# Eight pairs of buffers for split weight parts instead of seven, in a two-layer fp32 block on one core

## The chip, the core and the metric

The kernel runs on one core of a Trainium2 chip. The metric is device time in microseconds (us), from one launch on the inputs of the reference. Times of several runs are given as a median with the lowest and the highest.

## What is computed

The reference is two layers of a hybrid block on an activation `x` of 256 rows by 1024 columns in float32. Cut to what matters:

```
def hybrid_layer(x, ...):
    proj = rms_norm(x, g_mix_norm) @ w_in
    m_qk, m_v, m_o, m_i, m_f, moba_qkv, cq, ckv, kpe = split(proj)
    hm = mlstm_chunkwise(...)            # 4 heads, chunks of 64
    ha = moba_attention(...)             # 4 heads of 64, one block of 256
    hl = causal_block_attention(...)     # 4 heads, latent q and k, v
    x = x + concat([hm, ha, hl]) @ w_out
    h2 = rms_norm(x, g_mlp_norm)
    return x + square(relu(h2 @ w_up)) @ w_down     # 1024 -> 4096 -> 1024
```

All weights are float32 and come from memory once; together with the small inputs the run reads 113 MB.

## The kernel before

Every large product is made from split operands. A float32 number is written as a high part in TensorE's reduced float32 format plus a low part, and `mm3` (L249 to L252) issues three matmuls for each product: high by high, low by high, high by low. In the profile they are lines 250, 251 and 252 (405, 407 and 410 where a first block is put in another order). So each weight has to be split on its way:

- `load` (L192 to L201) fetches a job of up to 2048 columns x 128 partitions (1 MB) into one of three `raw` buffers, on SyncE's queue.
- `stream` (L203 to L227) cuts the job into pieces of up to 1024 columns. ScalarE writes the high part `wh` (L217), VectorE the low part `wl` by a subtraction (L225). For every fourth `up` piece of the MLP, VectorE is spared: ScalarE writes the negated high part into `wl` (L220), and GpSimd issues a transfer that adds the weights from memory to it (L222).
- `dn_part` (L229) gives the pieces of the down projection. For the first 14 of its 16 blocks four matrices are used, a (512 columns), b, d and c (1024 each), where d and c are sums that VectorE makes (`tsum`, L238 to L240); seven products of them, in the order a, b, d, c, d, c, b, stand for eight. The last two blocks take two pieces, e and b.
- `weights` (L244) is called where a piece is used. It splits ahead of that use:

```
    def stream(i):
        while state["split"] < min(i + SPLIT_AHEAD + 1, len(pieces)):
...
                h = hlp.tile([128, PW], F32R, name="wh", tag="wh")
                lo = hlp.tile([128, PW], F32R, name="wl", tag="wl")
```

The pool `hlp` has `SPLIT_AHEAD + 1` buffers of each of `wh` and `wl` (4096 bytes a partition each), the pool `rawp` has `DMA_AHEAD + 1`. A piece can be split once the piece that had its buffers has been used for the last time.

A layer runs through stages (projections, three kinds of attention, the output projection) in an order written out in `ORDERS` (L30). The program gives the order in which stages are recorded; a scheduler then sets the order of the instructions on each engine, from its own model of their durations. Where one stage ends and the next begins, `last_rows` updates the halves of `xs` one by one (L940 after the output projection, L988 after the MLP), and `transposer` (L388) with `transposed` transposes them on TensorE into `xtp` (L384), which ScalarE and VectorE split into `xh` (L376) and `xl` (L378); `first_blocks` (L398) holds the first matmuls on them.

The MLP loop (L992 to L1039) runs over 16 blocks of 256 hidden columns. In each round two `up` pieces are used for one bank `up`, ScalarE takes relu (`rr`, L1009) and square (`us`, L1010), VectorE makes three sums (L1012 to L1014), ScalarE and VectorE split the result into `hrh` (L1019) and `hrl` (L1020), and TensorE makes the products of the block two rounds back (`LAG`), P1 to P7.

In the middle of a layer, `lkl` (L710) is the normalised latent key on VectorE, `ltp` (L721) its transposes on TensorE, `scr` (L748) a square on ScalarE that reads the bank of the projection `pp`, and `qkp` and `vp` are further projections.

Of the kernel before, what the change touches and what calls it, by code (L numbers as in the profile page):

```python
# [23 lines left out]
RW = 2048  # L24
PW = 1024
DMA_AHEAD = 2
SPLIT_AHEAD = 6
LAG = 2

ORDERS = [o.split() for o in ("""  # L30
# [108 lines left out]
def hybrid_kernel(ctx: ExitStack, tc: tile.TileContext, x: bass.AP, xt: bass.AP, pos: bass.AP,  # L139
# [5 lines left out]
    rawp = ctx.enter_context(tc.tile_pool(name="raw", bufs=DMA_AHEAD + 1))  # L145
    hlp = ctx.enter_context(tc.tile_pool(name="hl", bufs=SPLIT_AHEAD + 1))
    tb = ctx.enter_context(tc.tile_pool(name="tb", bufs=1))
# [55 lines left out]
    def stream(i):  # L203
        while state["split"] < min(i + SPLIT_AHEAD + 1, len(pieces)):
            _, pc, j, c, n = pieces[state["split"]]
            while state["dma"] < min(j + DMA_AHEAD + 1, len(jobs)):
                next(load(state["dma"]))
                state["dma"] += 1
            r = raw[j][:, c:c + n]
            if pc[0] == "dn":  # L210
                r = dn_part(j, pc[2])
            if j == 0:
                hl[state["split"]] = (r,)
            else:
                h = hlp.tile([128, PW], F32R, name="wh", tag="wh")
                lo = hlp.tile([128, PW], F32R, name="wl", tag="wl")
                A.activation(h[:, :n], r, AF.Copy)  # L217
                if pc[0] == "up" and pc[1] % 4 == 3:

                    A.activation(lo, h.bitcast(F32), AF.Copy, scale=-1.0)  # L220
                    m, o = jobs[j]
                    G.dma_start(lo, bass.AP(tensor=wts.tensor, offset=wts.offset + o + c, ap=[[m, 128], [1, n]]),  # L222
                                accum_op=OP.add)
                else:
                    V.tensor_sub(lo[:, :n], r, h[:, :n].bitcast(F32))  # L225
                hl[state["split"]] = (h, lo)
            state["split"] += 1  # L227
# [895 lines left out]
```

## Time and profile before

| what | value |
|---|---|
| median of 3 runs | 600.15 us (599.92 to 601.45) |
| the profiled execution's own time | 601.67 us |
| its span, first to last instruction | 599.9 us |
| granted TensorE clock | 1.00 in every stretch (2.4 GHz) |
| busy: TensorE, its weight loads, VectorE, ScalarE, GpSimd | 98%, 87%, 86%, 70%, 9% |
| chain that ended last: TensorE, DMA, VectorE, ScalarE | 81%, 7%, 6%, 4% |
| software-made transfers (GpSimd's queue) | 2304 packets, 8.39 MB |

The span is 1.8 us shorter than the execution's own time. Busy shares are means over stages: the MLP loop, which runs from about 140 to 300 us and from about 430 to 590 us, is denser on VectorE than the attention stages. Matmuls overlap their neighbours, so their printed durations are longer than their pace; the pace is read from the starts of neighbours. A wait in the lists is idle time of the engine that ended when the named work was done.

### The profile page before, as it was taken

What the parts mean: (1) busy time and instruction counts of PE and PEld (TensorE: products, weight loads), DVE (VectorE), ACT (ScalarE), POOL (GpSimd) and SP (SyncE); (2) the same over time, 40 slices, a digit from 0 to 9 for tenths busy, and PEclk for the clock granted to TensorE, in tenths of its full rate; (3) what the DMA queues carried; (4) which work ended last, traced back from release to release, by engine and by line L of the source; (5) the groups of instructions that cost most, each with busy time, mean ns of one, the idle gap of its engine ahead of it and who ended that gap; (6) DMA issues with size and microseconds to landing.
All of it is one profiled execution on the core that took longest, in us unless ns stands there. A gap on an engine that the chain in (4) does not pass through costs nothing.

```text
span 599.9 us, 10005 instructions
## 1 busy us (share of the span) xinstructions
PE 585.6 (98%) x3766; PEld 523.8 (87%) x3766; DVE 516.2 (86%) x951; ACT 418.7 (70%) x671; POOL 54.6 (9%) x107
## 2 busy tenths in 40 slices
PE   6998999999999999999999999999999999999997
PEld 5987878889998898989889897888899899998985
DVE  4789895767999999999788997785789999999975
ACT  4785785557877778768657787563687787778670
POOL 7972000000000000000000000000000000000000
PEclk9999999999999999999999999999999999999999
DMA  8786321464676777678537623326656786778631
GB/s 292 280 290 235 101 109 43 175 207 141 186 243 210 243 243 232 223 230 257 191 110 253 235 82 133 107 71 205 180 159 227 204 267 214 215 227 243 219 101 70
DMA packets 19632, 114.78 MB, mean 191 GB/s; under 512 B 2560, under 2 KB 3072, under 8 KB 7808
## 3 DMA queue, kind: packets, MB, share of 16 engines
q1 hardware_dynamic: 16992, 105.75, 50.5%
q0 software_dynamic: 2304, 8.39, 7.7%
q8 instruction: 29, 0.48, 0.3%
q14 instruction: 19, 0.16, 0.1%
q10 hardware_dynamic: 288, 0.02, 0.0%
HBM read 113.09 MB, written 1.05 MB: 190 GB/s over the span
## 4 chain that ended last, share of the span: by engine, by line
PE 81%; DMA 7%; DVE 6%; ACT 4%; issue 1%; SPq 0%; DVEq 0%
PE up L251 8%; PE up L250 8%; PE up L252 8%; PE P L252 7%; PE P L251 7%; PE P L250 7%; DMA wl<-in_wts_dram 5%; DVE wl L225 3%; PE acc L250 2%; PE acc L252 2%; PE acc L251 2%; ACT wh L217 2%; PE latp L562 2%; DMA raw<-in_wts_dram 1%; PE vp L251 1%
## 5 line engine op out<-in xcount | busy, mean ns | idle before, releaser
L217 ACT ACTIVATE wh<-raw 128x1024 fp32r<-128x1024 f32 (+2 forms) x196 | 190.1, 981 | 72.6 <-PE acc L251 18.8
L225 DVE TENSOR_TENSOR wl<-raw,wh 128x1024 fp32r<-128x1024 f32 (+4 forms) x180 | 200.5, 1120 | 35.3 <-ACT wh L217 31.0
L251 PE MATMUL up<-xh,wl 128*128 128x256 f32 x480 | 133.8, 279 | 1.0 <-DMA wl<-in_wts_dram 1.0
L250 PE MATMUL up<-xh,wh 128*128 128x256 f32 x480 | 133.4, 278 | 0.9 <-DVE xl L378 0.9
L252 PE MATMUL up<-xl,wh 128*128 128x256 f32 x480 | 132.9, 277 | 0.0
L251 PEld LDWEIGHTS up<-xh,wl 128*128 128x128 f32 x480 | 90.3, 188 | 3.2 <-DMA wl<-in_wts_dram 1.8
L250 PEld LDWEIGHTS up<-xh,wh 128*128 128x128 f32 x480 | 90.1, 188 | 2.5 <-issue 1.4
L252 PEld LDWEIGHTS up<-xl,wh 128*128 128x128 f32 x480 | 90.2, 188 | 0.0
L252 PE MATMUL P<-wl,hrh 128*128 128x512 f32 x228 | 89.9, 394 | 0.0
L251 PE MATMUL P<-wh,hrl 128*128 128x512 f32 x228 | 89.5, 393 | 0.0
L250 PE MATMUL P<-wh,hrh 128*128 128x512 f32 x228 | 88.7, 389 | 0.0
L225 DVE TENSOR_TENSOR wl<-tsum,wh 128x1024 fp32r<-128x1024 f32 x56 | 66.2, 1218 | 0.4 <-ACT wh L217 0.4
L217 ACT ACTIVATE wh<-tsum 128x1024 fp32r<-128x1024 f32 x56 | 56.3, 1046 | 2.8 <-PE P L252 1.5
L222 POOL DMA_DIRECT2D wl<-in_wts_dram x16 | 14.0, 874 | 482.1 <-ACT wl L220 400.8
L251 PEld LDWEIGHTS P<-wh,hrl 128*128 128x128 f32 x228 | 42.8, 188 | 8.8
L252 PEld LDWEIGHTS P<-wl,hrh 128*128 128x128 f32 x228 | 42.9, 188 | 8.6
L250 PEld LDWEIGHTS P<-wh,hrh 128*128 128x128 f32 x228 | 42.8, 188 | 8.4
L1009 ACT ACTIVATE rr<-up 128x512 f32<-128x512 f32 x32 | 19.1, 597 | 34.8 <-PE up L252 34.8
L1019 ACT ACTIVATE hrh<-us 128x896 fp32r<-128x896 f32 (+1 forms) x32 | 29.1, 910 | 16.4 <-DVE us L1014 16.4
L238 DVE SCALAR_TENSOR_TENSOR tsum<-raw 128x1024 f32<-128x1024 f32 x28 | 34.1, 1219 | 6.2 <-DMA raw<-in_wts_dram 6.2
L1020 DVE TENSOR_TENSOR hrl<-us,hrh 128x896 fp32r<-128x896 f32 (+1 forms) x32 | 33.3, 1040 | 2.0 <-ACT hrh L1019 2.0
L250 PE MATMUL acc<-wh,mh 128*128 128x512 f32 x64 | 25.6, 400 | 0.0
(368 smaller groups left out, 1141.6 us busy)
## 6 DMA issues: line engine op xcount, KB each, us to landing
raw<-in_wts_dram SPq DMA_DIRECT2D x91, 1024.0 KB, 4.9
wl<-in_wts_dram POOLq DMA_DIRECT2D x16, 512.0 KB, 7.5
raw<-in_wts_dram SPq DMA_DIRECT2D x2, 740.0 KB, 5.0
raw<-in_wts_dram SPq DMA_DIRECT2D x2, 576.0 KB, 5.4
xts<-in_xt_dram SPq DMA_DIRECT2D x4, 256.0 KB, 4.6
raw<-in_wts_dram SPq DMA_DIRECT2D x4, 256.0 KB, 4.9
xs<-in_x_dram SPq DMA_DIRECT2D x1, 1024.0 KB, 10.0
raw<-in_wts_dram SPq DMA_DIRECT2D x2, 512.0 KB, 3.5
```

Source lines behind the costliest of these rows:

```text
L217: A.activation(h[:, :n], r, AF.Copy)
L222: G.dma_start(lo, bass.AP(tensor=wts.tensor, offset=wts.offset + o + c, ap=[[m, 128], [1, n]]), accum_op=OP.add)
L225: V.tensor_sub(lo[:, :n], r, h[:, :n].bitcast(F32))
L238: V.scalar_tensor_tensor(t[:, :1024], r[:, :1024], -1.0, r[:, 512:1536], op0=OP.mult, op1=OP.subtract)
L250: T.matmul(o, lh, rh, start=start, stop=False, **kw)
L251: T.matmul(o, ll, rh, start=False, stop=False, **kw)
L252: T.matmul(o, lh, rl, start=False, stop=stop, **kw)
L562: T.matmul(first[b], part(b, k)[0], xts[:, k], start=k == 0, stop=k == KT - 1))
L1009: A.activation(r, up, AF.Relu)
L1019: A.activation(hh, src, AF.Copy)
L1020: V.tensor_sub(hlo, src, hh.bitcast(F32))
```

## The change

```
-SPLIT_AHEAD = 6
+SPLIT_AHEAD = 7
...
-    nc = _bacc.Bacc("TRN2", target_bir_lowering=False, num_devices=1)
+    nc = _bacc.Bacc("TRN2", target_bir_lowering=False, num_devices=1, dynamic_dma_scratch_size=8192)
```

The pool of split parts gets an eighth pair of buffers, 2 x 4096 bytes a partition. They are taken from the area in on-chip memory that is kept for the descriptors of GpSimd's transfers, which goes from 16384 to 8192 bytes. No instruction is added or removed. The scheduler orders TensorE's, ScalarE's and VectorE's instructions anew from about 41 us on; on GpSimd and SyncE the order is the same.

In the MLP loop, ScalarE, the round that ends with GpSimd's seventh accumulating transfer (numbers are those of the buffers). Before:

```order
L1009 ACTIVATE rr_1605<-up_2765 128x512
L217 ACTIVATE wh_2833<-raw_2722 128x512
L1010 ACTIVATE us_1607<-rr_1605 128x512
L217 ACTIVATE wh_2840<-raw_2722 128x1024
L1019 ACTIVATE hrh_1610<-us_1607 128x896
L217 ACTIVATE wh_2851<-tsum_2847 128x1024
L217 ACTIVATE wh_2858<-tsum_2847 128x1024
L217 ACTIVATE wh_2877<-raw_2766 128x1024
L217 ACTIVATE wh_2905<-raw_2766 128x1024
L220 ACTIVATE wl_2906<-wh_2905 128x1024
```

The same round after the change:

```order
L1009 ACTIVATE rr_1611<-up_2771 128x512
L217 ACTIVATE wh_2837<-raw_2691 128x1024
L1010 ACTIVATE us_1613<-rr_1611 128x512
L217 ACTIVATE wh_2848<-tsum_2844 128x1024
L217 ACTIVATE wh_2855<-tsum_2844 128x1024
L217 ACTIVATE wh_2864<-raw_2753 128x1024
L217 ACTIVATE wh_2881<-raw_2753 128x1024
L1019 ACTIVATE hrh_1616<-us_1613 128x896
L220 ACTIVATE wl_2882<-wh_2881 128x1024
L217 ACTIVATE wh_2912<-raw_2800 128x512
```

The pieces there are a (512 columns), b, d and c (from `tsum`) and two `up` pieces. Part a has moved from the round's start to the end of the round before, and `hrh` from between b and d to behind both `up` pieces. On VectorE the order of the round has become b, d, c with one sum behind each, then the `up` pieces, `hrl`, a and the sums of `tsum`.

At the step from the output projection to the MLP (layer 0), VectorE, from the last update but one of `xs` on. Before:

```order
L940 TENSOR_TENSOR xs<-xs,acc 128x512
L240 TENSOR_TENSOR tsum<-tsum,raw 128x512
L378 SCALAR_TENSOR_TENSOR xl<-xtp,par_77,xh 128x256 x2
L225 TENSOR_TENSOR wl<-raw,wh 128x1024
L378 SCALAR_TENSOR_TENSOR xl<-xtp,par_77,xh 128x256 x2
L940 TENSOR_TENSOR xs<-xs,acc 128x512
```

After the change:

```order
L940 TENSOR_TENSOR xs<-xs,acc 128x512 x3
L378 SCALAR_TENSOR_TENSOR xl<-xtp,par_77,xh 128x256 x2
L225 TENSOR_TENSOR wl<-raw,wh 128x512
L378 SCALAR_TENSOR_TENSOR xl<-xtp,par_77,xh 128x256 x2
L940 TENSOR_TENSOR xs<-xs,acc 128x512
```

The first three updates now stand together, and the split between the two pairs of `xl` is one of 512 columns. ScalarE's order there has changed in the same way, and layer 1 has the same change.

At the boundary between the layers, VectorE, around the updates of `xs` from P4 and P2. Before:

```order
L225 TENSOR_TENSOR wl_3352<-raw_3279,wh_3351 128x1024
L988 SCALAR_TENSOR_TENSOR xs_81<-P4_1877,r2_1603,xs_81 128x512
L988 SCALAR_TENSOR_TENSOR xs_81<-P2_1849,r2_1603,xs_81 128x512
L225 TENSOR_TENSOR wl_3359<-raw_3279,wh_3358 128x1024
L988 SCALAR_TENSOR_TENSOR xs_81<-P5_1881,r2_1603,xs_81 128x512
```

After the change:

```order
L225 TENSOR_TENSOR wl_3356<-raw_3276,wh_3355 128x1024
L988 SCALAR_TENSOR_TENSOR xs_81<-P4_1883,r2_1609,xs_81 128x512
L225 TENSOR_TENSOR wl_3365<-raw_3292,wh_3364 128x888
L988 SCALAR_TENSOR_TENSOR xs_81<-P2_1853,r2_1609,xs_81 128x512
L988 SCALAR_TENSOR_TENSOR xs_81<-P5_1887,r2_1609,xs_81 128x512
L988 SCALAR_TENSOR_TENSOR xs_81<-P3_1891,r2_1609,xs_81 128x512
```

A split of 888 columns, which had its place behind all of these, now stands between P4's and P2's update.

In the middle of layer 0, TensorE has five matmuls of `qkp` and seven of `vp` more ahead of the transposes of `lkl`, and VectorE has two splits of 1024 columns more and four small operations fewer ahead of `lkl`; the seven last transposes of the latent query now stand ahead of the wait on `scr`. In layer 1 the middle is nearly unchanged.

## Rows read from the trace of the kernel before

**Rows 1.** The page, part 1: busy us (share of the span) xinstructions.
```profile
PE 585.6 (98%) x3766; PEld 523.8 (87%) x3766; DVE 516.2 (86%) x951; ACT 418.7 (70%) x671; POOL 54.6 (9%) x107
```

**Rows 2.** List of waits, TensorE: waited for, us in total, times, longest.
```profile
PE latp L562 <- DMA raw<-in_wts_dram: 5.6, 1, 5.6
PE ltp L721 <- DVE lkl L710: 1.4, 1, 1.4
PE up L251 <- DMA wl<-in_wts_dram: 1.0, 3, 0.5
PE up L250 <- DVE xl L378: 0.9, 2, 0.5
PE qkp L250 <- ACT scr L748: 0.7, 1, 0.7
```

**Rows 3.** Windows: us; busy of PE, PEld, DVE, ACT, POOL; clock; DMA share; GB/s.
```profile
230.00:260.00 30.00, 30.00 (x203) 27.48 (x202) 29.62 (x38) 24.21 (x30) 1.71 (x2) 1.00 0.71 231
```

**Rows 4.** Timeline, TensorE: start, us, engine, line, operation [idle before, releaser].
```profile
262.88 0.28 PE L252 MATMUL up<-xl,wh 128*128 128x256 f32 x1
262.99 0.28 PE L250 MATMUL up<-xh,wh 128*128 128x256 f32 x1
263.80 0.38 PE L251 MATMUL up<-xh,wl 128*128 128x256 f32 x1 [0.54 <-DMA wl<-in_wts_dram]
```

**Rows 5.** Line 222: who waited for it, and its transfers' time to landing.
```profile
PEld up L251: 1.8, 4
...
DMA to landing us min/median/max: 5.4/7.5/8.4
```

**Rows 6.** Timeline, GpSimd: the seventh accumulating transfer.
```profile
255.37 0.86 POOL L222 DMA_DIRECT2D wl<-in_wts_dram  x1 [19.69 <-ACT wl L220]
```

**Rows 7.** Timeline, ScalarE: the round before that transfer.
```profile
245.36 0.60 ACT L1009 ACTIVATE rr<-up 128x512 f32<-128x512 f32 x1 [1.66 <-PE up L252]
...
248.89 0.95 ACT L1019 ACTIVATE hrh<-us 128x896 fp32r<-128x896 f32 x1 [0.94 <-DVE us L1014]
249.75 1.99 ACT L217 ACTIVATE wh<-tsum 128x1024 fp32r<-128x1024 f32 x2
...
252.92 1.06 ACT L217 ACTIVATE wh<-raw 128x1024 fp32r<-128x1024 f32 x1 [0.23 <-PE up L252]
254.01 1.06 ACT L220 ACTIVATE wl<-wh 128x1024 fp32r<-128x1024 f32 x1
```

**Rows 8.** Timeline, VectorE: the subtraction of the first up piece.
```profile
253.16 1.22 DVE L225 TENSOR_TENSOR wl<-raw,wh 128x1024 fp32r<-128x1024 f32 x1
```

**Rows 9.** Timeline, SyncE's queue: the weight load ahead of the transfer.
```profile
254.44 0.33 SPq L198 DMA_DIRECT2D raw<-in_wts_dram  x1
```

**Rows 10.** DMA packets, MB, share: 254.4 to 258.7 us, then 258.7 to 263.6.
```profile
q1 hardware_dynamic: 125, 1.00, 67.3%
...
q0 software_dynamic: 144, 0.52, 58.2%
```

**Rows 11.** Timelines, VectorE and TensorE: output projection to MLP, layer 0.
```profile
134.34 1.23 DVE L225 TENSOR_TENSOR wl<-raw,wh 128x1024 fp32r<-128x1024 f32 x1 [0.24 <-ACT wh L217]
135.48 0.87 DVE L378 SCALAR_TENSOR_TENSOR xl<-xtp,par,xh 128x256 fp32r<-128x256 f32 x2
...
136.50 0.36 PE L250 MATMUL up<-xh,wh 128*128 128x256 f32 x1 [0.45 <-DVE xl L378]
```

**Rows 12.** Timelines, VectorE and TensorE: the layer boundary.
```profile
302.32 1.40 DVE L988 SCALAR_TENSOR_TENSOR xs<-P,r,xs 128x512 f32<-128x512 f32 x2
...
303.77 0.88 PE L384 MATMUL xtp<-ck,xs 128*128 128x128 f32 x6 [0.22 <-DVE xs L988]
```

**Rows 13.** Timeline, ScalarE: the layer boundary.
```profile
302.37 1.89 ACT L217 ACTIVATE wh<-raw 128x1024 fp32r<-128x1024 f32 x2 [3.60 <-PE P L251]
```

**Rows 14.** Timelines, VectorE and TensorE: the middle of layer 0.
```profile
58.45 0.68 DVE L710 TENSOR_TENSOR lkl<-lkl,lks 128x512 f32<-128x512 f32 x1
...
59.18 1.08 PE L721 MATMUL ltp<-ck,lkl 128*96 128x128 f32 x8 [1.42 <-DVE lkl L710]
```

## The prediction

> **What bounds the kernel now.** I read the page's busy shares first: TensorE is busy 585.6 us of a span of 599.9 us, 98% [rows 1]. So nothing that happens on another engine is worth anything unless it takes away one of TensorE's waits or makes a new one, and all of its idle time is 599.9 - 585.6 = 14.3 us. The list of TensorE's waits says where the named part of it lies [rows 2]: 5.6 us is the first weight load at the start, which the change cannot reach, since the order of the instructions is the same up to about 41 us. What is left for a deeper ring of split weights is short: 1.4 us before the transposes of `lkl`, 1.0 us in three waits on the accumulating transfer of `wl`, 0.9 us in two waits on `xl`, 0.7 us on `scr`. Then I read the stretches [rows 3]. In the MLP loop between 230 and 260 us TensorE is busy 30.00 of 30 us, VectorE 29.62, ScalarE 24.21, all at a granted clock of 1.00. So the reader should see two things: the loop has at most its few waits to give, and VectorE, which makes the low parts, has 0.38 us of room in 30.
>
> **The change, part by part.** It adds no instruction and removes none; GpSimd's and SyncE's queues keep their order, so no transfer moves past another on its queue. What changes is how far ahead a piece may be split (the piece now waits for the last use of the eighth piece before it, not of the seventh) and the order that the scheduler makes of it on TensorE, ScalarE and VectorE. I cost four places.
>
> *1. The accumulating transfers in the MLP loop.* At 262.99 a matmul starts; its neighbours follow at a pace of 0.11 us, so the next, the first to read `wl`, is due at 263.10. It starts at 263.80, 0.70 us late [rows 4]. Counted like this from start to start, three more of the 16 transfers are waited for (0.43, 0.21 and 0.35 us), together 1.7 us; the lists say 1.0 us of waiting for matmuls [rows 2] and 1.8 us for weight loads [rows 5], which brackets that. The transfer is issued at 255.37 [rows 6], 10.0 us after `rr` at 245.36. ScalarE's rows show why so late [rows 7]: part d can only be split at 249.75, when the products that read the slot's old part b are over, then c and the first up block, the second up block at 252.92, and the negated copy at 254.01. With eight buffers d takes the slot of part a, which is free long before, and c becomes the one that waits for b until about `rr` + 4.4. From there c, two up blocks (0.95 us each from start to start), `hrh`, now behind them (0.86, its step in the same rows), and the negated copy (1.0) plus the 0.3 us from its end to the issue, make `rr` + 9.45: 0.55 us earlier. The weight load that goes out before it is released by the subtraction of the first up block, which ends at 254.29 [rows 8], and goes out at 254.44 [rows 9]. It too comes about 0.55 us earlier: VectorE, which works without a break, ends the three sums at `rr` + 7.2 when its operations are added up in the new order, and with 1.13 for the subtraction and 0.15 to the issue that is `rr` + 8.5 instead of 9.1. This matters, since none of the accumulating transfer's packets moves for 3.3 us after its issue, while the load ahead of it drains, and all 144 move after that [rows 10]. Both being earlier by 0.55 us, the landing is too: three waits vanish and the largest keeps 0.15 us. That gives -0.43 - 0.21 - 0.35 - 0.55 = **-1.5 us**. Bounds: 0, if the next load, which now also starts earlier, takes the bandwidth back (landing already spreads from 5.4 to 8.4 us [rows 5]); -1.7, all of it.
>
> *2. From the output projection to the MLP, once in each layer.* VectorE subtracts a 1024-column piece at 134.34, before the second pair of `xl` at 135.48; TensorE waits for that pair and goes on at 136.50 [rows 11]. In the new order a 512-column piece stands there. ScalarE makes its high part in some 0.55 us instead of about 1.0, and VectorE its low part in 0.6 instead of 1.14, so the pair ends about 0.8 us earlier, and TensorE's wait is shorter than that (0.9 us in two waits by the list, 0.66 and 0.71 from start to start). I take 0.55 each, nearer to the start-to-start figures: **-1.1 us**. Bounds -0.9 and -1.6 (the second counts 0.1 to 0.25 each for the update of `xs` ahead of it, which also moves up). No gain at all would need the cover to be elsewhere, and no row shows another wait there.
>
> *3. The layer boundary.* Now VectorE updates `xs` from P4 and P2 in one go from 302.32, and TensorE transposes P2's half at 303.77 [rows 12]. In the new order the subtraction of an 888-column piece stands between the two updates. Its high part goes into the slot for which ScalarE waits until 302.37 today [rows 13], so it is ready near 303.25, and the subtraction takes 1.0 us to 304.25. P2's update ends near 304.9 instead of 303.7, and TensorE has only transposes left. What is late next is the latent projection behind them, by the same amount: **+1.2 us**. Bounds 0 (ScalarE's slot comes free earlier than I read it) and +1.3.
>
> *4. The middle of layer 0.* TensorE stands at `lkl` until 59.18, since VectorE ends it at 59.13 [rows 14]. VectorE is continuously busy there, and the new order puts two more subtractions (1.13 each) and four fewer small operations (0.08 each) ahead of `lkl`: ready at about 61.1. TensorE meanwhile does 5 matmuls of 256 columns (0.11) and 7 of 512 columns (0.23) more, 2.17 us of work that came later before, and the 0.7 us wait on `scr` is filled by seven transposes that used to come after it, without changing the end. Net 61.1 - 59.1 - 2.17 = **-0.15 us**. The bound below is -2.2, the work if `lkl` came no later; above it is +1.0, half of that work gone missing as cover for the softmax that follows.
>
> Sum: -1.5 - 1.1 + 1.2 - 0.15 = -1.55 us. The profiled execution took 601.67 us, 1.5 us above the median of 600.15, so it would come to 600.1; from the median, **598.6 us**. This kernel's measurement tells about 0.3%, 1.8 us, from no change: the forecast lies just inside.
>
> **The rivals.** *A, every wait on a split goes.* The Trainium skill, Perfetto Trace Analysis, section Optimization Strategy, says that the same gap repeating on the engine that should be saturated can mean that there is not enough SBUF for the next tile. The trace bears it out only in part, since the gaps differ from transfer to transfer and 12 of the 16 show none. As a mechanism of this kernel: the splits run far enough ahead that the boundary piece is also split before P4, so place 3 costs nothing, and places 1, 2 and 4 give 1.7, 1.6 and 0.9: 600.15 - 4.2 = 596.0. Against it: the order on VectorE is fixed, and a piece that stands between two updates stays there.
>
> *B, the loop keeps its waits.* The earlier transfer meets the next load sooner and lands when it did; then -1.1 + 1.2 - 0.15 leaves 600.1. For it: the load after next is released by part b, which is now split first. Against it: the transfers that had a load right behind them did not all land late.
>
> *C, slower: VectorE becomes the bound of the loop.* It has 0.38 us of room in 30 [rows 3], 0.13 us per iteration of 10.27 us. `hrh` has moved behind both up blocks on ScalarE, so `hrl`, and everything behind it on VectorE, may wait. Every 0.1 us per iteration beyond 0.13 costs 28 x 0.1 = 2.8 us over both layers. By my working `hrh` ends at `rr` + 8.1 and VectorE reaches `hrl` after 8.4, so it does not wait; from a wait of 0.13 us on, this decides. At 0.3 us: 28 x 0.17 = 4.8, with place 1 lost and -0.05 from the others: 604.9.
>
> *D, the halved area makes GpSimd wait.* Then the issues, not the buffers, decide. At one more issue time each (0.86 us [rows 6]) in the some 14 iterations with a transfer, against 0.55 gained, at most 14 x 0.3 + 1.2 more waits: about 605. Against it: one transfer is in flight at a time, 144 packets or 9 per DMA engine. The Trainium skill, Debugging Trainium Hangs, section Descriptor Overflow, names too many descriptors for this area as a cause of hangs; no run here shows the area full.
>
> **How the numbers follow.** The forecast's case 0.50, A 0.14, B 0.22, C 0.10, D 0.04. The forecast's own range is 597.4 to 600.0; 0.22 of its chance lies below 598.35 (0.3% under the median) and the rest within. Faster: 0.22 + 0.14 = 0.36; same: 0.28 + 0.22 = 0.50; slower: 0.14. The range reaches from A to somewhat beyond B, with place 3 and 4 at their upper bounds and nothing gained in place 2: 596.0 to 601.5. It leaves out C and D.
>
> **What would show it.** Right: the waits of `up` on the DMA of `wl` are at most 0.3 us in all; the wait on `xl` at 136 and 429 us is gone; the transposes at 303.8 start near 305 relative to the last product, about 1.2 us later; the wait on `lkl` lengthens to some 2 us while that on `scr` shrinks; GpSimd issues 9.4 to 9.5 us after `rr`. Wrong: an idle VectorE before `hrl` (C), transfers that land as late after `rr` as before (B), or GpSimd busy longer than 0.9 us at line 222 (D).

## The result, and the profile after

The changed kernel takes 597.74 us (median of 13 runs, 597.31 to 600.81), the kernel before on the same chip 600.96 us (13 runs, 599.59 to 604.08). The ratio is 0.995, 95% interval 0.9937 to 0.9963: 0.5% faster, a little more than the 0.3% that counts as no change. Forecast were 598.6 us, with a range from 596.0 to 601.5.

The profiled execution of the changed kernel is a bad one of its kind: 600.81 us, span 599.0, where ten of the 13 runs have spans of 595.5 to 596.2. What sets it apart is TensorE's clock, for about 3 us in each of two places (at the end of this section). The page, parts 1 and 4:

```profile
PE 585.7 (98%) x3766; PEld 525.3 (88%) x3766; DVE 514.0 (86%) x951; ACT 418.6 (70%) x671; POOL 54.6 (9%) x107
...
PE 88%; POOL 5%; DVE 4%; issue 2%; ACT 1%; DVEq 0%; POOLq 0%
```

Against [rows 1] the work is the same, to within some 2 us on each engine. The chain of waits no longer goes through a DMA (7% before): no accumulating transfer is on it. The list of TensorE's waits:

```profile
PE latp L562 <- DVE xts L523: 5.7, 1, 5.7
PE ltp L721 <- DVE lkl L710: 1.7, 1, 1.7
PE xtp L384 <- DVE xs L988: 1.6, 1, 1.6
PE latp L405 <- ACT xh L376: 0.2, 1, 0.2
```

Against [rows 2]: the waits on `wl`'s transfers, on `xl` and on `scr` are gone, the one on `lkl` is 0.3 us longer, and a wait of 1.6 us on `xs` is new.

**The MLP loop.** ScalarE's timeline for a round like that of [rows 7]:

```profile
244.95 0.60 ACT L1009 ACTIVATE rr<-up 128x512 f32<-128x512 f32 x1 [2.09 <-PE up L252]
245.44 1.05 ACT L217 ACTIVATE wh<-raw 128x1024 fp32r<-128x1024 f32 x1
...
247.04 2.17 ACT L217 ACTIVATE wh<-tsum 128x1024 fp32r<-128x1024 f32 x2
249.11 1.99 ACT L217 ACTIVATE wh<-raw 128x1024 fp32r<-128x1024 f32 x2
251.18 0.96 ACT L1019 ACTIVATE hrh<-us 128x896 fp32r<-128x896 f32 x1
252.04 1.04 ACT L220 ACTIVATE wl<-wh 128x1024 fp32r<-128x1024 f32 x1
```

The timelines of VectorE, SyncE's queue and GpSimd in the same round, to be read beside [rows 6, 8, 9]:

```profile
251.01 1.22 DVE L225 TENSOR_TENSOR wl<-raw,wh 128x1024 fp32r<-128x1024 f32 x1
...
252.29 0.33 SPq L198 DMA_DIRECT2D raw<-in_wts_dram  x1
...
253.38 0.86 POOL L222 DMA_DIRECT2D wl<-in_wts_dram  x1 [19.69 <-DVE tsum L238]
```

From `rr` to the negated copy (L220), ScalarE stands still nowhere for more than some 0.1 us; before, it stood 0.94 us ahead of `hrh` and 0.23 us ahead of the second up piece [rows 7]. The weight load goes out at `rr` + 7.34 (252.29 - 244.95) instead of + 9.08, the accumulating transfer at + 8.43 instead of + 10.01.

The load is released by VectorE's subtraction of the first up piece in this round of both kernels: it goes out 0.15 us after VectorE has begun its next operation (254.29 before, 252.14 now). VectorE has no idle time of more than 0.04 us ahead of that in either round, so the load comes when the work that stands ahead of it is done. That was 7.80 us from `rr` to the start of the subtraction (253.16 - 245.36 [rows 7, 8]) and is 6.06 us now (251.01 - 244.95). Two operations that stood there before have gone behind it, part a (0.6 us from start to start) and `hrl` (1.0 us); VectorE's timeline before:

```profile
247.13 0.68 DVE L225 TENSOR_TENSOR wl<-raw,wh 128x512 fp32r<-128x512 f32 x1
...
249.88 1.09 DVE L1020 TENSOR_TENSOR hrl<-us,hrh 128x896 fp32r<-128x896 f32 x1
```

The packet records show the accumulating transfer's first packet at 256.37 and its last at 260.40, `rr` + 15.45, where TensorE wants it at about `rr` + 17.7 (263.10 - 245.36 before). Over all full rounds the last packet comes at `rr` + 14.9 to + 16.5, before at + 16.2 to + 18.1. So nobody waits, though the time from issue to landing (line 222) is no better than in [rows 5]:

```profile
DMA to landing us min/median/max: 5.5/7.3/9.1
```

Every full round takes 10.27 us, and from the first product of the down projection to the last, each loop takes 149.11 us; before, 151.04 and 150.46. That is -1.93 and -1.35, together **-3.3 us**.

**From the output projection to the MLP.** Timelines of VectorE and TensorE, layer 0, against [rows 11]:

```profile
134.80 0.69 DVE L225 TENSOR_TENSOR wl<-raw,wh 128x512 fp32r<-128x512 f32 x1
135.41 0.87 DVE L378 SCALAR_TENSOR_TENSOR xl<-xtp,par,xh 128x256 fp32r<-128x256 f32 x2
...
136.68 0.37 PE L250 MATMUL up<-xh,wh 128*128 128x256 f32 x1
```

The small split stands in the place of the large one, the second pair of `xl` follows 0.61 us after its start instead of 1.14, and TensorE does not stop. From the last matmul of `acc` to the first product of the MLP it is 17.86 us in both layers; before, 18.26 and 18.76: **-1.3 us**.

**The boundary of the layers.** Timelines of TensorE, VectorE and ScalarE, against [rows 12, 13]:

```profile
301.40 0.40 PE L252 MATMUL P<-wl,hrh 128*128 128x512 f32 x1
...
303.69 0.88 PE L384 MATMUL xtp<-ck,xs 128*128 128x128 f32 x6 [1.58 <-DVE xs L988]
304.81 0.58 PE L405 MATMUL latp<-xh,wh 128*128 128x256 f32 x1 [0.24 <-ACT xh L376]
...
300.87 0.74 DVE L988 SCALAR_TENSOR_TENSOR xs<-P,r,xs 128x512 f32<-128x512 f32 x1
301.89 1.08 DVE L225 TENSOR_TENSOR wl<-raw,wh 128x888 fp32r<-128x888 f32 x1 [0.28 <-ACT wh L217]
302.89 2.06 DVE L988 SCALAR_TENSOR_TENSOR xs<-P,r,xs 128x512 f32<-128x512 f32 x3
...
300.92 1.53 ACT L217 ACTIVATE wh<-raw 128x888 fp32r<-128x888 f32 x2 [3.48 <-PE P L251]
```

Between the update from P4 and the others stands the subtraction of 888 columns, and VectorE even waits 0.28 us for its high part. From the last product to the next layer's first projection it is 3.41 us (304.81 - 301.40) instead of 2.04: **+1.4 us**.

**The middle of layer 0.** TensorE's timeline, against [rows 14]:

```profile
60.81 1.08 PE L721 MATMUL ltp<-ck,lkl 128*96 128x128 f32 x8 [1.67 <-DVE lkl L710]
```

From the first transpose of the latent query to that of `lkl`, the five profiles made with the new order here (the changed kernel and experiments 2, 3, 5 and 7: 12.19 to 12.98 us) have a mean of 12.72 us, the four with the old (the kernel before and experiments 1, 4 and 9: 9.92 to 11.07) one of 10.49. The difference, 2.23 us, is the work that moved ahead (2.17) and 0.1. The execution's own spread there is 1 us, so this place is nothing that can be measured. Nor is anything lost behind it: from the first transpose of the latent query to the last matmul of `acc` it is 84.1 to 85.4 us with the old order and 84.3 to 85.1 with the new, without the profile of the changed kernel, where the clock falls: **about 0**.

**The clock.** Windows; after the busy times stand the granted clock, the DMA share and GB/s:

```profile
59.00:61.00 2.00, 0.33 (x3) 0.19 (x3) 2.00 (x14) 0.00 (x0) 0.00 (x0) 1.00 0.98 414
...
63.00:65.00 2.00, 2.00 (x10) 1.85 (x10) 1.61 (x11) 0.53 (x2) 0.00 (x0) 0.50 0.88 270
...
303.00:304.00 1.00, 0.31 (x3) 0.31 (x4) 1.00 (x2) 0.00 (x0) 0.00 (x0) 1.00 0.90 369
...
305.00:308.00 3.00, 3.00 (x15) 3.00 (x16) 2.39 (x6) 2.92 (x7) 0.00 (x0) 0.50 0.09 33
```

After each of the two waits of 1.6 to 1.7 us TensorE works for about 3 us at 0.50, the lower level of 1.2 GHz, which costs some 1.5 us each time: from the latent projection to its transposes in layer 1, which the change leaves alone, it is 40.48 us here and 38.96 before. With these 3.1 us taken off, the span is 595.9 us like the other runs', 4.0 below the 599.9 of before; the places above make -3.3 - 1.3 + 1.4 = -3.2, and the rest lies ahead of the output projection of layer 0, where these two executions differ by 0.2 us one way and 0.8 the other.

### The profile page after: what moved, and what is told of

It is laid out like the page before. It is cut to its first block, busy times and chain, and to the rows that moved or that the text cites. A ratio compares the mean times of both kernels' runs of the same rounds, so it can differ in the third digit from the quotient of the medians.

```text
span 599.0 us, 10036 instructions
## 1 busy us (share of the span) xinstructions
PE 585.7 (98%) x3766; PEld 525.3 (88%) x3766; DVE 514.0 (86%) x951; ACT 418.6 (70%) x671; POOL 54.6 (9%) x107
## 4 chain that ended last, share of the span: by engine, by line
PE 88%; POOL 5%; DVE 4%; issue 2%; ACT 1%; DVEq 0%; POOLq 0%
PE up L250 9%; PE up L251 9%; PE up L252 9%; PE P L252 9%; PE P L251 9%; PE P L250 9%; PE acc L250 2%; PE acc L252 2%; PE acc L251 2%; DVE wl L225 2%; PE op L250 1%; PE op L252 1%; PE op L251 1%; PE vp L252 1%; PE vp L251 1%
## 5 line engine op out<-in xcount | busy, mean ns | idle before, releaser
L217 ACT ACTIVATE wh<-raw 128x1024 fp32r<-128x1024 f32 (+2 forms) x196 | 187.2, 978 | 61.9 <-PE acc L251 16.9
L225 DVE TENSOR_TENSOR wl<-tsum,wh 128x1024 fp32r<-128x1024 f32 x56 | 68.2, 1218 | 5.1 <-ACT wh L217 5.1
L217 ACT ACTIVATE wh<-tsum 128x1024 fp32r<-128x1024 f32 x56 | 59.1, 1058 | 7.0 <-PE up L410 4.0
L238 DVE SCALAR_TENSOR_TENSOR tsum<-raw 128x1024 f32<-128x1024 f32 x28 | 34.1, 1217 | 0.3 <-DMA raw<-in_wts_dram 0.2
```

What stands on the lines that cost most here:

```text
L238: V.scalar_tensor_tensor(t[:, :1024], r[:, :1024], -1.0, r[:, 512:1536], op0=OP.mult, op1=OP.subtract)
```

## The experiments

The theory from this profile: **the order** that the eighth pair brings, with `hrh` and `hrl` behind the splits, is what frees the loop. The rivals: the buffer as such, or the smaller area. All ratios are to the kernel before on the same chip, with 95% intervals.

**1. The area alone.** Seven pairs, the orders of the kernel before.

```diff
-    nc = _bacc.Bacc("TRN2", target_bir_lowering=False, num_devices=1)
+    nc = _bacc.Bacc("TRN2", target_bir_lowering=False, num_devices=1, dynamic_dma_scratch_size=8192)
```

> Seven buffers as before, only the descriptor area halved; every engine's order is that of the kernel before. If the eighth buffer (with the order that it allows) is the cause, this is the kernel before: 600 to 601.5 us, ratio 1.000 within 0.002, waits of up on the accumulating transfer as before (about 1 us in matmuls, 1.8 us in weight loads). If a smaller area by itself speeds up or slows down GpSimd's transfers, the time from issue to landing at line 222 leaves its 7.5 us median and the ratio leaves 1 by over 0.003.

Measured: 601.61 us (12 runs) against 601.42, ratio 0.9995 (0.9981 to 1.0008). The area by itself does nothing; it is only the room for the eighth pair.

**2. A quarter of the area.** The changed kernel with `dynamic_dma_scratch_size=4096`.

> The changed kernel with an area of 4096 bytes instead of 8192; every engine's order is that of the changed kernel. If the area never binds: as the changed kernel, 597.3 to 598.2 us in most executions, ratio to the kernel before about 0.995, landing at line 222 about 7.3 us after issue, line 222 busy 0.86 us. If GpSimd has to wait for room in a small area, line 222 or its queue takes longer and the waits of up on the transfer come back: 1 us or more.

Measured: 599.2 us, ratio 0.9952 (0.9935 to 0.997), GpSimd's issues 856 to 1067 ns. Rival D is out: half or a quarter of the area holds these transfers without a wait.

**3. Eight pairs with `hrh` ahead of d.** In the changed kernel the split of d is tied behind `hrh` on ScalarE, as it stood before (an order of issue, no wait on data).

```diff
-                A.activation(hh, src, AF.Copy)
+                state["hrh"] = A.activation(hh, src, AF.Copy)
...
-                A.activation(h[:, :n], r, AF.Copy)
+                w_ = A.activation(h[:, :n], r, AF.Copy); (pc[0] == "dn" and pc[2] == "d" and "hrh" in state) and tc.add_manual_dep(w_.ins, state["hrh"].ins.name, ..., reason="order")
```

> Eight buffers, but on ScalarE the split of part d is tied behind hrh, as it stood before the change. If the gain in the MLP loop comes from the eighth buffer alone, the transfers are still issued some 8.4 us after rr, and no wait of up on them comes back: as the changed kernel, ratio 0.995. If it comes from hrh no longer standing ahead of d, c and the up pieces (hrh waits for VectorE's sums until about rr + 3.5), the issue goes back to rr + 9.5 to 10.1, and 1 to 2.7 us of waits come back: ratio 0.997 to 0.9995.

Measured: 629.52 us (6 runs), ratio 1.0449 (1.0421 to 1.0477), far more than either theory gave. TensorE's list of waits, then the timelines of ScalarE and SyncE's queue in one round:

```profile
PE up L251 <- DMA wl<-in_wts_dram: 22.1, 12, 3.0
...
252.57 0.60 ACT L1009 ACTIVATE rr<-up 128x512 f32<-128x512 f32 x1 [3.77 <-PE up L252]
...
257.95 0.95 ACT L1019 ACTIVATE hrh<-us 128x896 fp32r<-128x896 f32 x1 [3.31 <-DVE us L1014]
...
263.50 0.33 SPq L198 DMA_DIRECT2D raw<-in_wts_dram  x1
```

`hrh` waits 3.31 us for VectorE's sum, and everything behind it on ScalarE with it; the load goes out at `rr` + 10.93, the transfer lands at + 20.1. Eight pairs are no help in this order. (The tie made the scheduler place VectorE's sums anew too, so this is not the order of before with a buffer more, and its size says nothing of that.)

**4. Seven pairs with `hrh` and `hrl` late.** In the kernel before, with its area, the two are recorded a round later, and `hrh` is tied behind the split of the second up piece (the edit, cut).

```diff
+        def split_h(j, behind):
+            hh, hlo, src = late.pop(j)
+            w_ = A.activation(hh, src, AF.Copy)
+            if behind:
+                tc.add_manual_dep(w_.ins, state["u"].ins.name, ..., reason="order")
+            V.tensor_sub(hlo, src, hh.bitcast(F32))
+            hs[j] = (hh, hlo)
...
+                if j:
+                    split_h(j - 1, True)
```

> Seven buffers and the old area, but hrh is tied behind the second up piece on ScalarE, as the change has it. If the order alone is the cause, d and c start near rr + 2.1 to 4 and the transfer is issued at about rr + 8.4: the waits of up on it go, 2.5 to 2.7 us, ratio 0.9955. If the number of buffers binds, the second up piece still waits for the first one's matmuls until rr + 7.5, hrh then stands ahead of the negated copy, the issue comes at rr + 10.5 to 10.9, later than before, and nearly every transfer is waited for: 3 to 10 us slower, ratio 1.005 to 1.017.

Measured: 597.69 us (12 runs, 596.94 to 601.1), ratio 0.9953 (0.9936 to 0.9969). TensorE's waits, ScalarE's round, the load and GpSimd's issue:

```profile
PE up L250 <- DVE xl L378: 1.0, 2, 0.5
PE up L251 <- DMA wl<-in_wts_dram: 0.4, 1, 0.4
...
245.88 0.60 ACT L1021 ACTIVATE rr<-up 128x512 f32<-128x512 f32 x1 [0.93 <-PE up L252]
...
249.11 2.01 ACT L217 ACTIVATE wh<-tsum 128x1024 fp32r<-128x1024 f32 x2 [0.64 <-PE P L251]
...
253.54 1.06 ACT L217 ACTIVATE wh<-raw 128x1024 fp32r<-128x1024 f32 x1 [1.47 <-PE up L252]
254.50 0.94 ACT L996 ACTIVATE hrh<-us 128x896 fp32r<-128x896 f32 x1
...
254.62 0.33 SPq L198 DMA_DIRECT2D raw<-in_wts_dram  x1
...
256.68 0.86 POOL L222 DMA_DIRECT2D wl<-in_wts_dram  x1 [20.10 <-DVE hrl L999]
```

This run speaks for the order. The second up piece still waits for its buffer, 1.47 us, and the transfer is issued *later* than before, `rr` + 10.80 against + 10.01. Yet its first packet is at 258.67 (before, 258.79 in a round that began 0.5 us earlier) and its last at `rr` + 16.9 against + 18.1; all but one wait on the transfers are gone. So the transfer's own issue does not set its landing. The weight load ahead of it goes out at `rr` + 8.74, 0.34 us earlier. Here it comes right behind ScalarE's second up piece (253.54 + 1.06), while VectorE's subtraction is over 0.9 us before: the missing buffer holds it. The earlier load explains a part of the 1.2 us; the transfer's packets also take less time from first to last (3.6 us in the mean of 12 transfers, 3.9 before), and why is not shown. Seven pairs with another order take the same time as the whole change, though the wait on `xl` stays.

The time shows this, the profile only in part. The profiled execution took 601.1 us, 3.4 more than the median, as a 256-column matmul takes 118 ns in its first loop instead of 113, and a round 10.48 us; TensorE then asks for each piece later, and missing waits prove less. In its second loop, at the usual pace, five of the six transfers of full rounds land at `rr` + 15.9 to + 16.2 and one is waited for; that loop takes 150.18 us, 0.3 less than before, 1.1 more than with the change.

**5. The boundary, one piece less ahead.** The changed kernel, where the splits recorded at the last down piece of layer 0 reach one piece less far:

```diff
-        while state["split"] < min(i + SPLIT_AHEAD + 1, len(pieces)):
+        while state["split"] < min(i + SPLIT_AHEAD + 1 - ((pieces[i][0] == 0 and pieces[i][1][:2] == ("dn", 15))), len(pieces)):
```

> The changed kernel, only that one piece less is split ahead while the last down block of layer 0 is recorded: on VectorE the 888-column subtraction stands behind the updates from P4, P2, P5 and P3 again. If place 3 of the prediction is right (the subtraction between the updates costs 1.2 us or more), TensorE's wait on xs at the boundary falls from 1.6 us to 0.3 at most, and the usual time from 597.6 to about 596.2 us, ratio 0.993; executions in which the granted clock falls after that wait should be rarer. If the wait only moves to the latent projection behind it, the time stays at 597.6.

Measured: 596.83 us (6 runs), ratio 0.9929 (0.9901 to 0.9956). The wait on `xs` is 0.2 us, and from the last product to the projection it is 2.03 us: the loss at the boundary is this one subtraction.

**6. The middle undone.** The same condition, with two pieces fewer ahead, in the stages `"a"` and `"b"` of layer 0; the two more subtractions ahead of `lkl` go back behind it.

> The changed kernel, only that the middle of layer 0 splits two pieces less ahead: 7 subtractions ahead of lkl again, as before the change. Against the profiles with the old order there (lkl at 58.2 us, with 12 matmuls less done) the changed order should cost 0.4 to 0.6 us: then 597.1 us, ratio 0.994. By the prediction's place 4 (a gain of 0.15 us from the changed order) it is 597.7, ratio 0.9952.

Measured: 601.24 us (12 runs, from 598.05), ratio 0.9989 (0.997 to 1.0007). This fell: no gain, but a loss. TensorE comes to `lkl` earlier and waits 1.9 us there, and 0.7 us on `wl` of another projection; in the profiled run the granted clock falls to 0.50 behind that wait. Three executions with a mean clock of 0.999 or 1.00 took 598.0 to 599.5 us, so a part of the loss is the clock. The extra splits ahead of `lkl` were not what cost time.

**7. The boundary, two pieces less ahead** (experiment 5 with `2 * (...)`).

> As e5, with two pieces less at the boundary: only two subtractions instead of three ahead of the update from P4, and the 888-column one behind all updates. If VectorE's queue ahead of P4 binds too, another 0 to 0.7 us less than e5: 595.5 to 596.2 us, ratio 0.992. If not, as e5.

Measured: 596.29 us (5 runs, 595.88 to 597.7), ratio 0.9914 (0.99 to 0.9927), the lowest of all kernels here and faster than both. TensorE's list, then its and VectorE's timelines at the boundary:

```profile
PE ltp L721 <- DVE lkl L710: 1.4, 1, 1.4
...
300.39 0.48 PE L252 MATMUL P<-wl,hrh 128*128 128x512 f32 x1
301.13 0.39 PE L405 MATMUL latp<-xh,wh 128*128 128x256 f32 x1 [0.26 <-ACT xh L376]
...
297.92 2.06 DVE L988 SCALAR_TENSOR_TENSOR xs<-P,r,xs 128x512 f32<-128x512 f32 x3
299.89 1.22 DVE L225 TENSOR_TENSOR wl<-raw,wh 128x1024 fp32r<-128x1024 f32 x1
```

Three updates of `xs` come ahead of the split, most transposes lie under the last products, and the projection starts 0.74 us after the last of them (3.41 in the changed kernel). The loop ahead is 0.8 us longer for it (149.92), so 1.9 of these 2.7 us are gained. The mean clock of this execution is 1.00.

**8. Work in front of the wait on `lkl`.** Experiment 7, and the first transpose of `lkl` tied behind five more matmuls of `vp`.

> As e7, and TensorE's transposes of lkl in layer 0 are tied behind five more matmuls of vp, which are ready while it waits. If that wait is idle time that any ready work fills, 1.1 us less than e7 (5 x 0.23): about 594.7 us, ratio 0.990. If those matmuls had been hiding the softmax behind lkl, a new wait of the same size comes there and the time stays that of e7.

Measured: 596.8 us (11 runs), ratio 0.9925 (0.9901 to 0.9949). The wait on `lkl` shrinks from 1.4 to 0.4 us, and a wait of 1.0 us on the softmax behind it is new (`at_pa`, L483): it moved, it was not filled.

**9. Seven pairs with `hrl` alone late.** In the kernel before, `hrh` keeps its place, `hrl` is recorded a round later and tied behind the first up piece's subtraction.

> Seven pairs and the old area; of the two parts of relu(h) that are added up late, only the low one, which VectorE computes, is recorded a round later, behind the first up piece's subtraction; the high one stays on ScalarE where the kernel before has it, ahead of d's split and behind the wait for the sum. If what delays the weight load of the next accumulating transfer is VectorE's low part of 1.09 us standing ahead of the subtractions of d, c and the up pieces, the load goes out some 0.4 us earlier after the round's first relu than before (about 8.7 us instead of 9.08), ScalarE's second up part then being what it waits for, still held by its buffer at about 7.6 us; most waits of TensorE on the accumulating transfers go, the loops come out near 149.3 us each, and the ratio to the kernel before is 0.995 to 0.997. If it is the high part's wait on ScalarE, which moves d, c and both up parts, the load stays at about 9 us, 6 to 9 waits remain, and the ratio is 0.999 to 1.001.

Measured: 647.63 us (6 runs), ratio 1.0766 (1.0739 to 1.0794). A miss for both theories, since the edit did not stay where it was meant. In ScalarE's timeline, 6.93 us after that round's `rr` at 254.91:

```profile
261.84 2.01 ACT L217 ACTIVATE wh<-tsum 128x1024 fp32r<-128x1024 f32 x2 [1.63 <-DVE tsum L240]
```

The scheduler filled `hrl`'s place on VectorE with the sums that make d and c (L238 to L240), so d and c are split late, the load goes out at `rr` + 11.58 (266.49), the transfer lands at + 19.6, and TensorE waits 30.6 us for 12 of the 16. Whether `hrh`'s place or `hrl`'s weighs more stays open. That a late load makes a late landing is seen once more.

**10. Nine pairs**, an area of 2048, and the boundary as in experiment 7.

> Nine pairs, an area of 2048 bytes, and at the end of layer 0 two pieces fewer ahead, as in the version with eight pairs that came out at 596.3. If more buffers help as such, the loops lose nothing against eight pairs (149.1 us each) and the time is 595.5 to 596.5, ratio 0.990 to 0.992. If the order that the pairs bring decides, then in the rounds where the high part of relu(h) comes ahead of c's split again the round's load is released later (over 8 us after the round's first relu instead of 7.3), the transfer lands past 16 us after it, TensorE waits again, and the time is 598 or more. If an area of 2048 bytes no longer holds a transfer of 144 descriptors, or those of two transfers, GpSimd's issue of it gets longer than 0.9 us and the loops get slower by over 3 us, whatever the order.

Measured: 599.59 us (12 runs), ratio 0.9971 (0.9956 to 0.9985): 3.3 us slower than with eight pairs (ratio 0.9914 there). GpSimd's issues take 853 to 1065 ns, so the area is not it. The loops take 151.27 and 149.77 us (149.92 and 149.11 in experiment 7), the middle is 1.6 us longer. ScalarE's `rr` and the load after it, in an early and a late round of layer 0:

```profile
161.85 0.60 ACT L1009 ACTIVATE rr<-up 128x512 f32<-128x512 f32 x1 [1.66 <-PE up L252]
...
169.46 0.33 SPq L198 DMA_DIRECT2D raw<-in_wts_dram  x1
...
244.04 0.60 ACT L1009 ACTIVATE rr<-up 128x512 f32<-128x512 f32 x1 [1.58 <-PE up L252]
...
252.86 0.33 SPq L198 DMA_DIRECT2D raw<-in_wts_dram  x1
```

The load slips from `rr` + 7.61 to + 8.82 in eight rounds, 0.15 us a round, while TensorE's rounds still take 10.27; then the transfer lands at `rr` + 18.4, and TensorE waits. In this order VectorE does a round's three small sums one behind the other, which takes 1.00 us from start to start instead of 0.74 with splits between them. Whether VectorE thus becomes the bound, as rival C had it, one pair further on, is not shown: between 200 and 241 us it still stands idle for 0.24 us a round (0.30 in the changed kernel).

**11. Eight pairs, but splits recorded six pieces ahead.** The constant sets both the number of pairs and the distance; here they are apart, in the kernel before with the area of 8192:

```diff
-    hlp = ctx.enter_context(tc.tile_pool(name="hl", bufs=SPLIT_AHEAD + 1))
+    hlp = ctx.enter_context(tc.tile_pool(name="hl", bufs=SPLIT_AHEAD + 2))
```

> The constant of the change sets two things: how many pairs the pool has, and how many pieces ahead of a use the program records a split. Here the pool has eight pairs (area 8192) and the splits are recorded six pieces ahead, as in the kernel before. The order of the MLP loop is then the one of the changed kernel, and at the boundary no subtraction stands between the updates of xs from P4, P2, P5 and P3. If the loop's gain comes with the pool's eighth pair (through the order that it makes) and the boundary's loss with the longer distance, the loops take 149.1 us each from the first product to the last, from the last product to the next layer's first projection it is 2.0 us or less (3.4 in the changed kernel), and the time is 596.0 to 597.0, ratio 0.991 to 0.993. If the loop needs the longer distance too, its loops take 150 us or more and the time is 598 to 600.

Measured: 596.97 us (6 runs, 596.55 to 597.81), ratio 0.9924 (0.9908 to 0.9939). TensorE's and VectorE's timelines at the boundary:

```profile
299.53 0.40 PE L252 MATMUL P<-wl,hrh 128*128 128x512 f32 x1
...
301.56 0.38 PE L405 MATMUL latp<-xh,wh 128*128 128x256 f32 x1 [0.24 <-ACT xh L376]
...
298.99 2.72 DVE L988 SCALAR_TENSOR_TENSOR xs<-P,r,xs 128x512 f32<-128x512 f32 x4
```

The loops take 149.1 us each, as in the changed kernel, and all four updates of `xs` stand together; the boundary takes 2.03 us. The loop's gain comes with the pool's eighth pair, the boundary's loss with the longer distance. In the middle of layer 0 its order is another too: 82 matmuls and transposes from the first transpose of the latent query to that of `lkl` (75 before, 87 after the change). Its time cannot be told from experiment 7 (the intervals overlap).

## Why the prediction was right or wrong

| place | forecast | measured |
|---|---|---|
| 1 transfers in the loop | -1.5 (0 to -1.7) | -3.3 |
| 2 output projection to MLP | -1.1 | -1.3 |
| 3 boundary of the layers | +1.2 | +1.4 |
| 4 middle of layer 0 | -0.15 | about 0 |

The time came out 0.9 us under the forecast and in the range, and the sign was right; but the likeliest verdict was "within 0.3%", and it is faster by 0.5%. That the time is so near is partly luck: the kernel before took 600.96 us over 13 runs and not the 600.15 of the three that the forecast starts from, so the change itself is -3.2 us where -1.55 was forecast. Nearly all of this is place 1.

*Place 1, the step that failed.* "Bounds: 0 ... -1.7, all of it." It was not all of it. Counted from start to start over both loops of the kernel before, seven steps carry a wait, 1.86 us; in eight places the step behind such a late transfer is about 0.11 us longer as well, together 0.87 us; smaller delays make the rest of the 3.3. I had counted only the waits of the largest transfers.

The working under it failed too, in both of its terms. For the load it says that VectorE "ends the three sums at `rr` + 7.2 when its operations are added up in the new order". They end at `rr` + 6.06, since part a and `hrl` no longer stand ahead, and so the load goes out 1.74 us earlier, not 0.55. For the issue I wrote that "d can only be split at 249.75, when the products that read the slot's old part b are over", and let c wait for b with eight pairs. But the row I quoted it from says what ended the idle time ahead of `hrh`: 0.94 us for VectorE's sum [rows 7]. `hrh` stood ahead of d, and d, c and both up pieces waited behind it; the buffer showed only in the 0.23 us of the second up piece. In experiment 4, with seven pairs as well, d does wait for its slot, but only until `rr` + 3.2, and not + 4.4. After the change c starts at 248.15, 3.2 us after `rr`, without the wait "until about `rr` + 4.4", and the issue comes 1.57 us earlier.

What is shown of the cause: with seven pairs the order is enough for the time (experiment 4), and with eight the pool's eighth pair brings that order (experiment 11). That eight pairs do nothing under the old order is not shown, since the tie of experiment 3 moved VectorE's sums as well. Whether `hrh` on ScalarE or `hrl` on VectorE held the load is open too: `hrl` stands ahead of the subtraction by VectorE's order and cannot start before `hrh` is done, and experiment 9 failed to part them.

What the step had right: the weight load ahead decides when the packets start, "none of the accumulating transfer's packets moves ... while the load ahead of it drains" [rows 10]. In all 13 traces the first packet came 3.8 to 4.7 us after the load's issue, wherever between 0.2 and 2.6 us behind it GpSimd's own issue lay. The Trainium skill, DMA: Bandwidth & Descriptors, section Queues, rings and completion order, has each DMA engine change between the rings it has work for, packet by packet. Within these 4 us the trace shows no such sharing; behind them it does. From 258.7 to 263.6 us in the kernel before, 90 packets of weight loads move beside the transfer's 144:

```profile
q1 hardware_dynamic: 90, 0.63, 35.0%
```

*Place 2* was right in mechanism and size: 0.55 us in each layer were forecast, 0.40 and 0.90 measured (the old order takes 18.3 or 18.8 us there in either layer, from profile to profile), and 512 columns in the place of 1024 is what the rows show.

*Place 3* was right, step by step: the 888 columns between the updates, 1.08 us, TensorE with "only transposes left", the projection later by as much. Experiments 5, 7 and 11 take it away again.

*Place 4* was right as "nearly nothing" and for its reason: `lkl` comes later by about as much as the work that moved ahead of it. Experiment 6 put the work back and lost. The price it has is another, which no step named: a longer wait can be followed by a fall of the clock.

*The rivals.* A (every wait goes, 596.0) was right in that every wait on the transfers goes, and wrong of the boundary. Experiments 7 and 11 measured 596.3 and 597.0, near A's number, but by another way: they split less far ahead at the boundary, not further, and A priced the loop at 1.7 and not 3.3. Its rule is that of the Trainium skill, Perfetto Trace Analysis, section Optimization Strategy, on equal gaps that can mean too little room for buffers. More room did remove the gaps here; but experiment 4 removed nearly all of them without it, and experiment 10 has more and gets some of them back. B was wrong: the loads that now go out earlier took back little, as the transfers' packets take 4.1 us from first to last in the mean of 12, before 3.9. C did not come, since `hrl` waited for nothing at eight pairs; whether it came at nine is open. D is excluded by experiments 1, 2 and 10.

## What to carry to other kernels

When idle time stands in front of an instruction, read what ended it before reading which buffer is scarce: an instruction that waits on another engine holds everything behind it in its engine's order, and moving it may be worth what another buffer is worth. Where an engine has no idle time ahead of an instruction that others wait for, add up what stands ahead of it in its order, from start to start. A constant that sets both the size of a pool and the distance ahead should be split in two and each tried alone. And measure what waits cost from stage to stage, since the lists of waits gave 1.0 to 1.8 us where 3.3 were to be had.

## What was unexpected of the hardware

- TensorE's granted clock fell to 0.50 for about 3 us after a wait of 1.6 to 1.9 us, and cost some 1.5 us, nearly as much as the wait. It did so in some executions and not in others: in the profiles of experiments 3, 5 and 10 waits of 1.6, 1.8 and 1.7 us have no fall behind them. In experiment 7, where the longest such wait is 1.4 us, the mean clock was 0.999 or 1.00 in four of the five runs; where the fifth (0.997) lost it is not known.
- In the loops of the kernel before, the step behind a late accumulating transfer takes about 0.11 us more than its neighbours (113 ns become 220), in eight places.
- None of an accumulating transfer's packets moved for 3.8 to 4.7 us from the issue of the weight load ahead of it; after that, they and those of the next load moved side by side.
- In one execution of experiment 4 the whole loop of layer 0 ran at 118 ns for a matmul of 256 columns instead of 113, with no waits and a granted clock of 1.00, so that rounds took 10.48 instead of 10.27 us; the loop of layer 1 ran at 113. Its cause stays open.
